# Forgetting attention rewritten as 64 steps of one row tile of two heads, with a fixed order on three engines

## The chip, the cores and the metric

The kernel runs on one core of a Trainium2 chip, as a single launch. The metric is the device time of that launch in microseconds (us). The core has the engines TensorE (PE, with its weight loads shown apart as PEld), VectorE (DVE), ScalarE (ACT) and GpSimd (POOL), and SyncE (SP), which here issues transfers. ACT and POOL issue transfers too. Each engine works through its own instructions in order and waits on semaphores for the others.

## The reference, cut to what matters

The whole computation is a two-layer decoder trunk on 1024 tokens of 1024 features, in float32: an RWKV-7 layer and a mixture of experts, then a "forgetting attention" layer and a second mixture of experts. The change lies in the attention layer, which has 16 heads of 64 features:

```
for i in range(S // Q_BLOCK):                       # 8 blocks of 128 rows
    lo, hi = i * Q_BLOCK, (i + 1) * Q_BLOCK
    logits = (einsum('bhqd,bhkd->bhqk', q[:, :, lo:hi], k[:, :, :hi]) * scale
              + (fcum[:, :, lo:hi, None] - fcum[:, :, None, :hi]))
    causal = (lo + arange(Q_BLOCK))[:, None] >= arange(hi)[None, :]
    logits = where(causal, logits, -inf)
    p = softmax(logits, axis=-1)
    outs.append(einsum('bhqk,bhkd->bhqd', p, v[:, :, :hi]))
...
return (o * sigmoid(qg[..., D:])) @ w_o             # w_o is scaled by (1 + gt_m) afterwards
```

Row block i sees (i + 1) * 128 keys, so the work of a block grows eightfold from i = 0 to i = 7.

## The kernel before

The eight head pairs (`m` = 0 to 7, two heads `e` each) are worked one after another; a pair has two halves of four row blocks. For one row block of one head (`Attention.half`, lines 2119 to 2159):

- PE multiplies the queries with the keys (L2138, two passes that add a high and a low part) and adds the causal mask (L2141), into a PSUM tile `psc`, of which there are two (two banks each). This is called S below.
- DVE adds the forget sums `nf` to it, writes the logits into `lg` and takes the row minimum in the same instruction (L2144; the scores are negated, so the minimum is the maximum). This is called L. A tiny instruction subtracts and adds the row's own forget sum to that minimum (L2150).
- ACT takes the exponential with that minimum as bias, and the row sum (L2151).
- DVE takes the reciprocal of the sum (L2152) and scales the row (L2153).
- PE transposes the row in 128 x 128 tiles (L2158) into the PSUM tiles `ptr` (three of one bank), called T, and ACT copies them out to `pT` (L2159).

When two row blocks of both heads are done, PE multiplies `pT` with `v` (L2170, called V), which adds up in `po` (one bank); after two such groups DVE multiplies by the output gate into `oT` (L2174). `lg` has four buffers, `nf` three, `v` one, `pT` two for each head.

In the pairs m = 1 to 4, after each half, `Attention.weight` prepares one of eight 128-row blocks of the output weights: a transfer into `wor`, which takes one of the four `lg` buffers, POOL multiplies it by the gate row (L2186), ACT copies it to `woh` (L68) and POOL subtracts to `wol` (L69).

Nothing fixes the order by hand: the framework's list scheduler lays the instructions of the five engines out by its own estimate of time, and each engine then works through its list. Queries and keys are loaded from the POOL queue, `v`, `nf`, gates and weights from the SP queue. Ahead of the attention the gates are computed (`Qkv.gates`): their sigmoid tiles `gs` lie in a pool that is closed before the attention's pool, with `lg` in it, is opened in the same memory. Behind it `out1` multiplies `oT` with the weights.

## Time and profile before

| | us |
|---|---|
| median of 3 runs (3153.26 to 3163.05) | 3161.29 |
| the profiled execution | 3158.01 |
| its span | 3156.3 |
| PE, DVE, ACT, POOL busy over the span | 2885.3, 2409.2, 1701.7, 853.9 |
| the attention, from the first logits (2074.67) to the end (2357.50) | 282.83 |
| PE, PEld, DVE, ACT, POOL busy in it | 256.01, 179.47, 213.21, 191.47, 83.20 |

The attention is 9% of the span. The mean granted TensorE clock over the span is 0.949 of 2.4 GHz. A record of a matmul holds its way through the pipeline too, so records of neighbours overlap, and how fast PE gets through a row of them is read from the starts of the weight loads. An idle time in square brackets stands before the instruction, with what ended it.

### The profile page before, as it was taken

To read this page: it belongs to the slowest core of one execution; us is meant where nothing else is said; L and a number is where in the kernel's file an instruction comes from. 1 tells how busy PE (TensorE), PEld (TensorE's weight loads), DVE (VectorE), ACT (ScalarE), POOL (GpSimd) and SP (SyncE) were. 2 spreads that over 40 slices of the span, in tenths; PEclk is the share of its full clock that TensorE was granted. 3 is DMA by queue.
4 is the path that set the end of the run, shared out by engine and by line. 5 is a ranking of instruction groups with operands and counts; after the bars stand their busy time and mean duration, and the time that the engine had idled before them with its cause. 6 is when DMAs were issued, how large, how long until landed. Compare 5 with 4: busy or idle time off the path is not lost. (4 is left out here: it accounts for less than half of the span.)

```text
span 3156.3 us, 51219 instructions
## 1 busy us (share of the span) xinstructions
PE 2885.3 (91%) x19763; PEld 2209.3 (70%) x19763; DVE 2409.2 (76%) x3676; ACT 1701.7 (54%) x2563; POOL 853.9 (27%) x446
## 2 busy tenths in 40 slices
PE   7989997769997999999989999998999799999996
PEld 5658776657775677767758989865667577766773
DVE  7477558478777999999965544167767899999996
ACT  4432554333334777767754233256663477776774
POOL 4010316000002344444400033023303532224430
PEclk9989998689998999999999999999999899999998
DMA  6487673485534999999975745546644399999995
GB/s 207 143 269 248 207 233 109 117 174 133 134 104 180 374 383 390 376 349 361 384 288 174 221 138 204 164 120 159 173 103 181 129 388 388 383 365 348 367 380 222
DMA packets 362035, 771.12 MB, mean 244 GB/s; under 512 B 134723, under 2 KB 236315, under 8 KB 311742
## 3 DMA queue, kind: packets, MB, share of 16 engines
q1 hardware_dynamic: 277596, 630.23, 57.6%
q0 software_dynamic: 29104, 70.55, 7.6%
q10 hardware_dynamic: 55090, 67.04, 6.6%
q8 instruction: 157, 2.57, 0.3%
q14 instruction: 88, 0.72, 0.1%
HBM read 664.06 MB, written 120.18 MB: 248 GB/s over the span
## 5 line engine op out<-in xcount | busy, mean ns | idle before, releaser
L1392 DVE TENSOR_TENSOR mlo<-mraw,mhi 128x1024 fp32r<-128x1024 f32 x752 | 872.8, 1218 | 13.2 <-ACT mhi L1387 12.7
L1387 ACT ACTIVATE mhi<-mraw 128x1024 fp32r<-128x1024 f32 x752 | 748.4, 1052 | 190.3 <-PE pd L1484 97.3
L1364 POOL DMA_INDIRECT Yd<-yo,sidx x64 | 396.1, 6189 | 422.9 <-DVE yo L1512 415.4
L1936 PE MATMUL ptk<-wh,hhi 128*128 128x256 f32 x768 | 216.7, 289 | 10.8 <-ACT ksq L1948 6.3
L1936 PE MATMUL ptk<-wl,hhi 128*128 128x256 f32 x768 | 215.9, 285 | 0.0
L1484 PE MATMUL pg<-mhi,xTl 128*96 128x512 f32 x512 | 205.2, 401 | 4.9 <-DVE xTl L69 4.9
L1484 PE MATMUL pd<-mhi,hTh 128*96 128x512 f32 x512 | 207.8, 406 | 0.0
L1936 PE MATMUL ptk<-wh,hlo 128*128 128x256 f32 x768 | 207.3, 286 | 0.2 <-DVE hlo L69 0.2
L1484 PE MATMUL pg<-mhi,xTh 128*96 128x512 f32 x512 | 205.1, 401 | 0.5 <-ACT xTh L68 0.5
L1484 PE MATMUL pu<-mhi,xTh 128*96 128x512 f32 x512 | 204.6, 400 | 0.0
L1484 PE MATMUL pd<-mhi,hTl 128*96 128x512 f32 x512 | 204.4, 399 | 0.0
L1484 PE MATMUL pd<-mlo,hTh 128*96 128x512 f32 x512 | 203.4, 397 | 0.0
L1484 PE MATMUL pg<-mlo,xTh 128*96 128x512 f32 x512 | 203.2, 397 | 0.0
L1484 PE MATMUL pu<-mhi,xTl 128*96 128x512 f32 x512 | 202.2, 395 | 0.0
L1484 PE MATMUL pu<-mlo,xTh 128*96 128x512 f32 x512 | 201.3, 393 | 0.2 <-POOL mlo L69 0.2
L1936 PEld LDWEIGHTS ptk<-wh,hhi 128*128 128x128 f32 x768 | 146.9, 193 | 16.2 <-ACT ksq L1948 8.0
L1358 POOL DMA_INDIRECT xb<-Hd,gidx x64 | 75.7, 1183 | 283.8 <-PE pxt L1471 279.9
L2144 DVE CUSTOM_DVE_ANT_0 lg<-psc,nf 128x256 f32<-128x256 f32 (+7 forms) x128 | 95.3, 752 | 74.0 <-DMA G1d<-gs 44.9
L1936 PEld LDWEIGHTS ptk<-wl,hhi 128*128 128x128 f32 x768 | 148.2, 193 | 0.3 <-issue 0.2
L1936 PEld LDWEIGHTS ptk<-wh,hlo 128*128 128x128 f32 x768 | 142.8, 193 | 2.3 <-issue 1.7
L1512 DVE SCALAR_TENSOR_TENSOR yo<-pd,gtab,mgt 96x512 f32<-96x512 f32 x128 | 93.2, 742 | 28.4 <-PE pd L1484 27.8
L1484 PEld LDWEIGHTS pg<-mhi,xTl 128*96 128x96 f32 x512 | 83.8, 164 | 43.6 <-DVE xTl L69 7.0
(555 smaller groups left out, 6920.4 us busy)
## 6 DMA issues: line engine op xcount, KB each, us to landing
mraw<-in_moe_wgate_dram SPq DMA_DIRECT2D x128, 1024.0 KB
mraw<-in_moe_wup_dram SPq DMA_DIRECT2D x128, 1024.0 KB
mraw<-in_moe_wdown_dram SPq DMA_DIRECT2D x128, 1024.0 KB
adaw<-in_ada_w_dram SPq DMA_DIRECT2D x48, 512.0 KB
mraw<-in_ada_w_dram SPq DMA_DIRECT2D x32, 512.0 KB
Q<-Qd POOLq DMA_DIRECT2D x64, 256.0 KB, 5.7
adk<-in_ada_w_dram SPq DMA_DIRECT2D x16, 512.0 KB
adaw<-in_kv_ada_w_dram SPq DMA_DIRECT2D x16, 512.0 KB
```

What stands on the lines that cost most here:

```text
L1358: return g.nc.gpsimd.indirect_dma_start(out=X[0:SL], out_offset=None, in_=g.Hd[l][:, :], in_offset=bass.IndirectOffsetOnAxis(ap=idx[0:SL], ...
L1364: return g.nc.gpsimd.indirect_dma_start(out=g.Yd[l][:, :], out_offset=bass.IndirectOffsetOnAxis(ap=idx[0:SL], axis=0), in_=Yo[0:SL], in_of ...
L1387: self.ex.g.nc.scalar.activation(hi, raw, AF.Copy)
L1392: self.ex.g.nc.vector.tensor_tensor(lo, raw, hi.bitcast(F32), op=ALU.subtract)
L1484: self.g.nc.tensor.matmul(p, a[:, k, :], b[:, kk, s], start=(k == 0 and j == 0), stop=(k == n - 1 and j == len(tt) - 1))
L1512: self.g.nc.vector.scalar_tensor_tensor(yo[0:SL, s], p, gcol[0:SL], self.gt[0:SL, s], op0=ALU.mult, op1=ALU.mult)
L1936: nc.tensor.matmul(p[:, 0:KU], x[:, t * P:(t + 1) * P], w[:, k, :], start=(k == 0 and j == 0), stop=(k == KT - 1 and j == 2))
L2144: nc.vector.tensor_tensor_reduce(lg[:, 0:W].rearrange("p (s w) -> p s w", s=ns), sc[:, 0:ns, 0:w], nf[e][:, 0:W].rearrange("p (s w) -> p s ...
```

## The change

The attention becomes one loop over 64 steps (`Attention.run`). A step is one row block of both heads of a pair. Within `Order`, the instructions of PE, ACT and DVE keep the order in which the program writes them. A step works on its own block `u` and on the block of the step before, `before`:

- PE: S of both heads of `u`, T of `before`'s first head, half of a waiting V, T of `before`'s second head.
- ACT: the copies of `before`'s first head, both exponentials of `u`, the copies of `before`'s second head.
- DVE: a gate product that is due, L of both heads of `u`, one piece of the weights, then reciprocal and scaling of each head of `u`.

The subtract-and-add of the forget sum (old L2150) is gone; the exponential takes the minimum as it comes. The weights are gated and split on DVE (instead of POOL), with the copy still on ACT, one block in five steps, in parts of `oT` that are not written yet. `nf` has four buffers, `v` two; the sigmoid tiles of the gates take the slots of the attention's gate tiles. A triangle of ones for the forget sums moves into a scratch area. Everything ahead of the gates and behind the attention has its order unchanged, but for a few of the last rows of the program.

```diff
         self.load_q(m, 0)
-        v = lp.tile([P, NT, P], F32, name="v1")
-        nc.sync.dma_start(v, g.V1d[:, m * P:(m + 1) * P].rearrange("(t p) c -> p t c", p=P))
         nf = []
         for e in range(2):
-            n_ = lp.tile([P, T], F32, name="nf", bufs=3)
+            n_ = lp.tile([P, T], F32, name="nf", bufs=4)
             nc.sync.dma_start(n_, brow(g.Fd[2 * m + e:2 * m + e + 1, :], T))
             nf.append(n_)
-        self.k[m] = K, v, nf
+        self.k[m] = K, nf
+
+    def load_v(self, m):
+        self.v[m] = (self.lp, self.sp)[m % 2].tile([P, NT, P], F32, name="v1")
+        self.g.nc.sync.dma_start(self.v[m], self.g.V1d[:, m * P:(m + 1) * P].rearrange("(t p) c -> p t c", p=P))
...
+    def run(self, sp, ps, oT):
+        g = self.g
+        order = Order(g.tc, mybir.EngineType.PE, mybir.EngineType.Activation, mybir.EngineType.DVE)
+        self.sp, self.ps, self.oT = sp, ps, oT
+        before, side = None, self.weights()
+        self.load_v(0)
+        for m in range(KT):
+            for half in range(2):
...
+                for ii in range(4):
+                    if ii == 0:
+                        group = Ctx()
+                        group.gt, group.m, group.half = gt, m, half
+                    u = Ctx()
+                    u.m, u.half, u.ii, u.i, u.group = m, half, ii, half * 4 + ii, group
+                    with order:
+                        self.step(u, before, side)
+                    before = u
+        while before or self.todo or self.gated:
+            with order:
+                self.step(None, before, side)
+            before = None
+        assert next(side, 1)
+
+    def step(self, u, before, side):
+        if self.gated:
+            self.gated()
+            self.gated = None
+        if u:
+            for e in range(2):
+                self.scores(u, e)
+            for e in range(2):
+                self.logits(u, e)
+            next(side, None)
+        if before:
+            self.transposed(before, 0)
+        if u:
+            self.exponents(u, 0)
+        if self.todo:
+            self.todo.pop(0)()
+        if u:
+            self.exponents(u, 1)
+            for e in range(2):
+                self.scaled(u, e)
+        if before:
+            self.transposed(before, 1)
+            if before.ii % 2:
+                for part in range(2):
+                    self.todo.append(lambda part=part: self.values(before, part))
+
...
-                    lg = sp.tile([P, T], F32, name="lg", bufs=4)
-                    mx = sp.tile([P, 4], F32, name="mx", bufs=4)
-                    nc.vector.tensor_tensor_reduce(
-                        lg[:, 0:W].rearrange("p (s w) -> p s w", s=ns), sc[:, 0:ns, 0:w],
-                        nf[e][:, 0:W].rearrange("p (s w) -> p s w", s=ns), 1.0, 3.0e38, op0=ALU.add, op1=ALU.min,
-                        accum_out=mx[:, 0:1])
-
-                    ft = g.fc[:, i, h:h + 1]
-                    nc.vector.tensor_scalar(mx[:, 1:2], mx[:, 0:1], ft, ft, op0=ALU.subtract, op1=ALU.add)
-                    nc.scalar.activation(lg[:, 0:W], lg[:, 0:W], AF.Exp, bias=mx[:, 1:2], scale=-1.0, accum_out=mx[:, 2:3])
-                    nc.vector.reciprocal(mx[:, 3:4], mx[:, 2:3])
-                    nc.vector.tensor_scalar(lg[:, 0:W], lg[:, 0:W], mx[:, 3:4], None, op0=ALU.mult)
-                    for j0 in range(0, i + 1, 4):
-                        n = min(4, i + 1 - j0)
-                        p = ps.tr.tile([P, 4, P], F32, name="ptr")
-                        for j in range(n):
-                            nc.tensor.transpose(p[:, j, :], lg[:, (j0 + j) * P:(j0 + j + 1) * P], g.ident)
-                        nc.scalar.activation(pT[:, j0:j0 + n, iq * P:(iq + 1) * P], p[:, 0:n], AF.Copy)
...
+    def exponents(self, u, e):
+        lg, mx = u.lg[e]
+        self.g.nc.scalar.activation(lg[:, 0:u.W], lg[:, 0:u.W], AF.Exp, bias=mx[:, 0:1], scale=-1.0, accum_out=mx[:, 2:3])
+
+    def scaled(self, u, e):
+        lg, mx = u.lg[e]
+        self.g.nc.vector.reciprocal(mx[:, 3:4], mx[:, 2:3])
+        self.g.nc.vector.tensor_scalar(lg[:, 0:u.W], lg[:, 0:u.W], mx[:, 3:4], None, op0=ALU.mult)
+
+    def transposed(self, u, e):
+        g, nc, lg = self.g, self.g.nc, u.lg[e][0]
+        if u.ii % 2 == 0 and e == 0:
+            self.pT = [self.sp.tile([P, NT, 256], F32, name=f"pT{x}", bufs=2) for x in range(2)]
+        u.pT = self.pT
+        s = slice(u.ii % 2 * P, u.ii % 2 * P + P)
+        for j0 in range(0, u.i + 1, 4):
+            n = min(4, u.i + 1 - j0)
+            p = self.ps.tr.tile([P, 4, P], F32, name="ptr")
+            for j in range(n):
+                nc.tensor.transpose(p[:, j, :], lg[:, (j0 + j) * P:(j0 + j + 1) * P], g.ident)
+            nc.scalar.activation(u.pT[e][:, j0:j0 + n, s], p[:, 0:n], AF.Copy)
+
...
+        for j in range(part * nj // 2, (part + 1) * nj // 2):
             t0 = max(0, j - nj + 2) * P
...
-            self.gate = sp.tile([P, D], F32, name="gate1")
-            nc.sync.dma_start(self.gate, brow(g.modr[M_GT1:M_GT1 + 1], D))
-            nc.gpsimd.tensor_scalar(self.gate, self.gate, 1.0, None, op0=ALU.add)
-        raw = sp.tile([P, D], F32, name="wor", tag="lg", bufs=4)
-        nc.sync.dma_start(raw, g.I["fx_wo"][0, k * P:(k + 1) * P, :])
-        nc.gpsimd.tensor_tensor(raw, raw, self.gate, op=ALU.mult)
-        w = [self.bp.tile([P, D], F32R, name=n, tag="hl", bufs=16) for n in ("woh", "wol")]
-        split(g, *w, raw, nc.gpsimd)
-        self.wo.append(w)
+        gate = self.oT[:, KT - 1]
+        nc.sync.dma_start(gate, brow(g.modr[M_GT1:M_GT1 + 1], D))
+        for k in range(KT):
+            hi, lo = (self.bp.tile([P, D], F32R, name=n, tag="hl", bufs=16) for n in ("woh", "wol"))
+            raw = self.oT[:, KT - 2 - (k % 2 and k < KT - 1)]
+            nc.sync.dma_start(raw, g.I["fx_wo"][0, k * P:(k + 1) * P, :])
+            self.wo.append([hi, lo])
+            yield
+            yield
+            if k == 0:
+                nc.vector.tensor_scalar(gate, gate, 1.0, None, op0=ALU.add)
+            nc.vector.tensor_tensor(raw, raw, gate, op=ALU.mult)
+            yield
+            nc.scalar.activation(hi, raw, AF.Copy)
+            yield
+            nc.vector.tensor_tensor(lo, raw, hi.bitcast(F32), op=ALU.subtract)
+            yield
...
-            with tc.tile_pool(name="gp", bufs=1) as sp:
-                for u in range(4):
-                    q.gates(sp, 12 + u, u)
-                    q.load()
+            for u in range(4):
+                q.gates(lp, 12 + u, u)
+                q.load()
...
-            for m in range(KT):
-                for half in range(2):
-                    if half == 0:
-                        at.load_q(m, 1)
-                    elif m + 1 < KT:
-                        at.load(m + 1)
-                    at.half(sp, ps, oT, m, half)
-                    if 1 <= m < 5:
-                        at.weight(sp, (m - 1) * 2 + half)
-            while at.late:
-                at.values(sp, ps, *at.late.pop(0))
+            at.run(sp, ps, oT)
```

ACT in the fourth pair (m = 3), from the exponentials of the row block with 640 keys. Before (`lg` logits, `pT` transposed rows, `woh` high part of the output weights):

```order
L2151 ACTIVATE lg,mx<-lg,mx 128x640 x2
L2159 ACTIVATE pT_20733<-ptr 128x4x128
L2159 ACTIVATE pT_20835<-ptr 128x4x128
L2159 ACTIVATE pT_20835<-ptr 128x128
L68 ACTIVATE woh<-wor 128x1024
L2151 ACTIVATE lg,mx<-lg,mx 128x768 x2
L2159 ACTIVATE pT_20836<-ptr 128x4x128
L2159 ACTIVATE pT_20836<-ptr 128x128
```

The same stretch now, up to the next weight copy:

```order
L2204 ACTIVATE lg,mx<-lg,mx 128x640 x2
L2222 ACTIVATE pT_20326<-ptr 128x4x128
L2222 ACTIVATE pT_20423<-ptr 128x4x128
L2222 ACTIVATE pT_20423<-ptr 128x128
L2204 ACTIVATE lg,mx<-lg,mx 128x768 x2
L2222 ACTIVATE pT_20424<-ptr 128x4x128
L2222 ACTIVATE pT_20424<-ptr 128x128
L2222 ACTIVATE pT_20423<-ptr 128x4x128
L2222 ACTIVATE pT_20423<-ptr 128x2x128
L2204 ACTIVATE lg,mx<-lg,mx 128x896 x2
```

The copy `woh` stood between two row blocks' exponentials and read what POOL had written; it now stands one block further on, ahead of the copies of the step, and reads what DVE wrote in the step before.

DVE at the last two row blocks of a pair. Before, in m = 5 (`mx` the minimum, the sum and its reciprocal, `g` the gate):

```order
L2144 ISA lg,mx<-psc,nf 128x896
L2144 ISA mx 128x1
L2150 TENSOR_SCALAR mx<-mx,fc 128x1
L2144 ISA lg,mx<-psc,nf 128x1024
L2144 ISA mx 128x1
L2150 TENSOR_SCALAR mx<-mx,fc 128x1
L2152 RECIPROCAL mx<-mx 128x1
L2150 TENSOR_SCALAR mx<-mx,fc 128x1
L2153 TENSOR_SCALAR lg<-lg,mx 128x896
```

Now, in m = 3, a step with a weight product in it (`oTt` on its own is the weight block):

```order
L2196 ISA lg,mx<-psc,nf 128x896
L2196 ISA mx 128x1
L2254 TENSOR_TENSOR oTt<-oTt 128x1024
L2208 RECIPROCAL mx<-mx 128x1
L2209 TENSOR_SCALAR lg<-lg,mx 128x896
L2208 RECIPROCAL mx<-mx 128x1
L2209 TENSOR_SCALAR lg<-lg,mx 128x896
L2237 TENSOR_TENSOR oTt<-po,g_20183 128x512
L2196 ISA lg,mx<-psc,nf 128x1024
```

Before, the logits of the next block stood between the logits and the scaling of this one. Now the scaling of both heads of a block comes before any logits of the next, and the weight product stands between the two.

PE at the row block with 896 keys. Before, in m = 6 (`psc` scores, `ptr` transposes, `po` values):

```order
L2138 MATMUL psc<-K_21619,Q_21860 128x384 x4
L2141 LDWEIGHTS identbf
L2141 MATMUL psc<-cmask,identbf 128x128
L2158 MATMUL ptr<-ident,lg 128x128 x12
L2170 MATMUL po<-pT_21930,v_21627 64x256
L2158 MATMUL ptr<-ident,lg 128x128
L2138 MATMUL psc<-K_21617,Q_21857 128x448 x4
L2141 LDWEIGHTS identbf
L2141 MATMUL psc<-cmask,identbf 128x128
L2170 MATMUL po<-pT_21931,v_21627 64x256
L2170 MATMUL po<-pT_21930,v_21627 64x256
```

Now, one step in m = 6:

```order
L2185 MATMUL psc<-K_21494,Q_21703 128x448 x4
L2188 LDWEIGHTS identbf
L2188 MATMUL psc<-cmask,identbf 128x128
L2221 MATMUL ptr<-ident,lg 128x128 x6
L2234 MATMUL po<-pT_21845,v_21506 64x256
L2234 MATMUL po<-pT_21846,v_21506 64x256
L2234 MATMUL po<-pT_21845,v_21506 64x128
L2234 MATMUL po<-pT_21846,v_21506 64x128
L2221 MATMUL ptr<-ident,lg 128x128 x6
L2185 MATMUL psc<-K_21492,Q_21700 128x512 x4
```

Scores, transposes of one head, values, transposes of the other head now follow one another in every step, where single value products and transposes stood between the scores before.

## Rows read from the trace of the kernel before

**Rows 1.** Windows, pairs m = 1 to 6; us, then PE, PEld, DVE, ACT, POOL busy, clock, DMA, GB/s

```profile
2101.04:2135.93 34.89, 33.68 (x242) 24.31 (x242) 27.74 (x87) 26.07 (x62) 10.71 (x12) 1.00 0.72 184
2135.93:2170.79 34.86, 30.56 (x210) 20.93 (x209) 28.61 (x79) 23.76 (x57) 15.79 (x14) 1.00 0.58 162
2170.79:2215.02 44.23, 34.95 (x218) 24.79 (x217) 26.83 (x82) 24.50 (x59) 15.59 (x14) 0.88 0.64 156
2215.02:2253.46 38.44, 33.09 (x218) 22.94 (x217) 29.21 (x82) 24.54 (x59) 16.08 (x14) 0.96 0.61 158
2253.46:2286.06 32.60, 30.50 (x208) 20.79 (x206) 25.02 (x81) 22.47 (x56) 11.17 (x12) 1.00 0.65 159
2286.06:2318.93 32.87, 30.47 (x212) 21.60 (x212) 24.55 (x82) 22.66 (x56) 4.88 (x8) 0.95 0.71 160
...
sum 282.83, PE 256.01 PEld 179.47 DVE 213.21 ACT 191.47 POOL 83.20; mean PE 32.00 PEld 22.43 DVE 26.65 ACT 23.93 POOL 10.40
```

**Rows 2.** Waits in the attention: who waited for whom, us in total, times, longest us

```profile
ACT woh L68 <- POOL wor L2186: 27.2, 8, 6.2
```

**Rows 3.** Timeline in pair m = 3: start, us, engine, what; idle before

```profile
2199.30 1.06 ACT L68 ACTIVATE woh<-wor 128x1024 fp32r<-128x1024 f32 x1 [4.25 <-POOL wor L2186]
2201.50 1.71 DVE L2153 TENSOR_SCALAR lg<-lg,mx 128x768 f32<-128x768 f32 x1
...
2203.32 1.14 PEld L2158 LDWEIGHTS ptr<-ident,lg 128*128 128x128 f32 x6 [4.84 <-ACT pT L2159]
```

**Rows 4.** Timeline at the start of the attention, ACT

```profile
2074.59 1.28 ACT L2151 ACT_TABLE_LOAD   x1 [2.33 <-DMA G1d<-gs]
```

**Rows 5.** Timeline in pair m = 2, PE's weight loads and one scaling

```profile
2155.01 1.49 PEld L2170 LDWEIGHTS po<-pT,v 128*64 128x64 f32 x14 [0.17 <-issue]
...
2162.10 0.61 DVE L2153 TENSOR_SCALAR lg<-lg,mx 128x768 f32<-128x768 f32 x1
...
2164.00 0.64 PEld L2158 LDWEIGHTS ptr<-ident,lg 128*128 128x128 f32 x6 [0.39 <-issue]
...
2164.61 0.76 PEld L2138 LDWEIGHTS psc<-K,Q 128*128 128x128 f32 x4
...
2165.65 0.10 PEld L2141 LDWEIGHTS <-identbf 128*128 128x128 bf16 x1 [0.28 <-issue]
...
2166.17 2.35 PEld L2170 LDWEIGHTS po<-pT,v 128*64 128x64 f32 x22
...
2174.62 0.30 PEld L2138 LDWEIGHTS psc<-K,Q 128*128 128x128 f32 x2 [1.54 <-DVE mx L2144]
...
2174.97 0.10 PEld L2141 LDWEIGHTS <-identbf 128*128 128x128 bf16 x1
```

**Rows 6.** Timeline in pair m = 7, PE's weight loads behind values

```profile
2327.21 0.14 PEld L2158 LDWEIGHTS ptr<-ident,lg 128*128 128x128 f32 x1 [0.38 <-issue]
```

**Rows 7.** Groups of instructions in the attention: busy us, mean ns, idle before

```profile
L2151 ACT ACTIVATE lg<-lg,mx 128x256 f32<-128x256 f32 (+7 forms) x128 | 98.6, 773 | 21.2 <-DVE mx L2150 15.5 <-DVE mx L2152 5.0
L2144 DVE CUSTOM_DVE_ANT_0 lg<-psc,nf 128x256 f32<-128x256 f32 (+7 forms) x128 | 95.3, 752 | 74.0 <-DMA G1d<-gs 44.9 <-PE ptr L2158 21.5 <-PE psc L2141 3.8
L2170 PE MATMUL po<-pT,v 128*64 128x256 f32 (+1 forms) x640 | 89.9, 373 | 9.8 <-DMA v<-V1d 5.3 <-ACT pT L2159 4.1
L2153 DVE TENSOR_SCALAR lg<-lg,mx 128x256 f32<-128x256 f32 (+7 forms) x128 | 77.2, 606 | 1.7
L2150 DVE TENSOR_SCALAR mx<-mx,fc 128x1 f32<-128x1 f32 x128 | 33.1, 266 | 0.8
L2152 DVE RECIPROCAL mx<-mx 128x1 f32<-128x1 f32 x128 | 20.2, 159 | 20.5 <-ACT lg L2151 19.7
L2174 DVE TENSOR_TENSOR oTt<-po,g 128x512 f32<-128x512 f32 x16 | 11.0, 688 | 17.5 <-PE po L2170 17.5
L68 ACT ACTIVATE woh<-wor 128x1024 fp32r<-128x1024 f32 x8 | 8.5, 1058 | 27.2 <-POOL wor L2186 27.2
```

**Rows 8.** Page, groups: a product of two 128 x 1024 tiles on DVE

```profile
L1392 DVE TENSOR_TENSOR mlo<-mraw,mhi 128x1024 fp32r<-128x1024 f32 x752 | 872.8, 1218 | 13.2 <-ACT mhi L1387 12.7
```

100 lines of the change are left out of this document (50 added, 50 removed).

## The prediction

> **What bounds the kernel now.** I read the windows of the attention first, one for each head pair. The reader is to see two kinds of pair [rows 1]. m = 5 and 6, in which no weights are prepared, take 32.60 and 32.87 us, and PE is busy in 30.5 of each. The four with weights take 34.89, 34.86, 44.23 and 38.44, 152.4 together, though PE and DVE have no more attention to do: against four pairs of 32.7 that is 21.6 us more. Eight pairs of 32.7 and these 21.6 make 283.2, which is the stretch's 282.83. So there are two quantities to work out, a pair without weights and the weights.
>
> The table of waits says what the weights cost: ACT stood 27.2 us in front of its eight copies `woh`, waiting for POOL [rows 2]. The timeline shows what that does to others [rows 3]. ACT idles 4.25 us before one `woh`, with the exponentials of the next row block queued behind it; PE's transposes then come 4.84 us late, and the six of them take 1.14 us where six take 0.64 elsewhere [rows 5], because the granted clock had fallen to 1.2 GHz in the idle time. The window of that pair has a mean clock of 0.88 [rows 1].
>
> The start is in the timeline too: the table load for the first exponential waits 2.33 us for the transfer that empties `gs` [rows 4], since `lg` lies in the memory of `gs`.
>
> **The change, part by part.**
>
> *PE in a pair.* The three kinds of work are the same as before, so I price them by the spacing of the weight loads where PE waits for nobody [rows 5]. T: 0.64 / 6 = 0.107 us a tile; a head has 36 tiles, a pair 72: 7.7 us. V: 2.35 / 22 = 0.107 a record; the 320 products show as 640 records [rows 7], 80 a pair: 8.6 us, or 0.9 less if the narrow products on the diagonal take half. S: for 512 columns from 2174.62 to 2174.97 + 0.10 = 0.45 us, for 2048 from 2164.61 to 2165.65 + 0.10 = 1.14. A line through both, over the 9,472 columns of a head's eight blocks, gives 8 x 0.45 + 5,376 x 0.45 / 1000 = 6.0, and 12.0 a pair. Together 28.3. The new order goes once in each step from T to V and once back. The first costs 0.17 [rows 5]; the second costs 0.38 in the one row I have [rows 6], and I let it go down to the 0.17 of the first: 8 x 0.34 to 8 x 0.55, 2.7 to 4.4. A pair then needs 31.0 to 32.7 of PE alone. I take 31.5, a little below the middle, since the upper end rests on that one row: 252 us for eight. A pair without weights gains only about 1.2 us by this.
>
> *DVE and ACT in a step.* The tiny instruction after L goes: 128 x 266 ns = 33.1 us of records [rows 7]; on DVE they overlap their neighbours, so it is worth less there, but in the chain of a row it stood in front of the exponential, and ACT waited 15.5 us for it. The new chain on DVE in a step is L, both exponentials, a reciprocal and the second scaling. Per pair, from the groups: 95.3 / 16 + 98.6 / 8 + 20.2 / 16 + the scaling. The scaling's 77.2 holds instructions slowed beside POOL, such as the 1.71 us for 768 columns [rows 3] that take 0.61 otherwise [rows 5]. POOL's sixteen products go, at most 1.1 us each, 17.6; I take 10, near the middle between none and that, so 67 / 16. With the gate product, 11.0 / 8, that is 6.0 + 12.3 + 1.3 + 4.2 + 1.4 = 25.2. Three handovers a step show no price of their own; between nothing and 0.17 each they add up to 4.1. So the chain needs 25 to 29 a pair, and PE's 31.5 lies above it: PE is the bound, if it gets to work a step ahead.
>
> The Trainium skill says on the page "SBUF — State Buffer", section "SBUF: two separate sides", that GpSimd and VectorE share a port pair as an exclusive lock and that the loser blocks for the whole instruction. By that rule all sixteen products held a scaling up and 17.6 come back; DVE would then have room for all of the weights, and the time would be 3133 instead of the 3139 below. The 1.71 is one such case; the 606 ns mean of the group is too low for every product to have cost a full one, so I keep 10.
>
> *The weights.* They leave POOL. ACT's 27.2 us of waiting goes, and with it the 21.6 us worked out above. What is late next is their work on DVE: sixteen products of 1.22 [rows 8] and one scalar addition, which at 0.61 x 1024 / 768 is 0.8: 20.3 us; ACT keeps its 8 x 1.06 = 8.5. If all of it lay on the path it would cost 28.8, if PE hides it nothing. It is spread over 40 steps, five pairs. PE's 31.5 leaves the middle of the chain, 27, about 4.5 a pair: 22.5 of room for 28.8. I take 6 on the path. On DVE the scalings are queued behind a product, and PE's transposes of the next step wait for those; a late transfer of a weight block would hold the whole step. Its issue lies eight steps ahead of its product from the third block on, at 3 to 4 us a step; of the first two blocks the product comes two and seven steps after, so one stall of a few us at the start is possible and is inside the bound.
>
> *Start and end.* With `gs` out of the way the first exponential comes 2.3 us earlier [rows 4]; the gates' last sigmoids on ACT and the last gate matmuls are then what is late. `nf` and `v` with one more buffer take away 5.3 us of PE's wait for `v` [rows 7]; that is inside the 32.7 and so inside the gain of a pair. Filling and emptying the pipeline of steps adds what PE waits in the first and last one: between 0 and 10, about three chains of 3.3; I take 5. Moving the triangle costs nothing: POOL makes it in both, far ahead of its use. Behind the attention the order is the same but for the last rows of the program; I cost that at 0, within 1 us.
>
> *Sum.* 252 + 6 + 5 = 263 against 282.8, that is 19.8 less, and 2.3 at the start: 22.1. The profiled execution took 3158.0 (span 3156.3), which becomes 3135.9. The median of the runs lies 3.3 above the profiled one: 3139.
>
> **The rivals.**
>
> *Everything hides (faster still).* Switches cost 0.17 each, narrow V products take half, the weights cost nothing, ends 2: 30.1 x 8 + 2 = 243, 42 less with the start, so 3119. For it: a steady order gives PE no long idle time, so the clock stays at 2.4 GHz. Against it: S, T and V would never wait for one another, and in the pairs without weights today PE still idles 2 us by its records [rows 1].
>
> *The weights only change engines (no change).* In a fixed order a product on DVE or a copy on ACT delays the scaling and so the next transposes each time, and all 28.8 lie on the path: 252 + 29 + 5 = 286, less 2.3, so 3162. For it: in a step with a product the chain (27 / 8 + 1.2 = 4.6) is longer than PE's mean step (31.5 / 8 = 3.9). Against it: the product stands where DVE waits for the exponential anyway.
>
> *PE never gets ahead (slower).* On ACT the exponentials of a step are queued behind the copies of the step before, those wait for transposes, and these stand on PE behind both scores of the step. The old list put the next block's logits into DVE's gaps; the new one can't. If PE starts a step's scores only when DVE is ready for them, a step's chain gets longer by one score, one head's transposes and a copy. By the rows that is 6.0 + 3.9 + 8 x 0.5 = 14 a pair; in half of the steps 7: 27 + 7 = 34 a pair, 272 + 29 + 5 = 306, 21 more with the start, so 3182. It decides from the point where ACT stands more than 0.6 us a step before its first copy. For it: ACT and DVE take their queues strictly in order, and [rows 3] shows a chain behind one late instruction. The skill's page "TensorE: Matmul & The Clock Gate", section on the array's architecture, says the same of both queues and that only PE can pull weight loads ahead; the trace agrees with the 4.84 us. Against it: two `psc` let PE run the next scores as soon as this step's logits are done, well ahead of the scalings.
>
> **How the numbers follow.** A change under 0.3%, 9.5 us, can't be told from none here. Forecast (12 to 32 us less) 0.53, everything hides 0.20, only change engines 0.15, never ahead 0.12. So faster 0.73, same 0.15, slower 0.12. The range goes from 3116, below the best case, to 3160, just short of the no-change case: it leaves out the slower case and part of the one before it.
>
> **What would show it.** Right: no wait of `woh` for POOL; PE's weight loads in a pair without weights spaced to 31 to 32 us; pairs with weights within 2 us of the others; the first logits 2 to 3 us after the last gate matmul; a granted clock of 1.0 in all pairs. Wrong: ACT idle before copies in most steps (never ahead); the first five pairs 4 us or more longer than the last three (only change engines); DVE waiting for a weight block's transfer; or a pair at 29 us or less, which would mean that today's spacing of PE's groups is not its floor.

## The result, and the profile after

The changed kernel takes 3115.32 us, the median of 4 runs (3110.18 to 3115.52), against 3159.8 for the kernel before beside it (4 runs, 3153.26 to 3163.05): ratio 0.9861, 95% interval 0.9843 to 0.9879. The forecast was 3139 with a range from 3116; the gain is twice the one forecast. The profiled execution took 3115.35 us (span 3113.6) against 3158.01: 42.7 less. The attention, from the first logits to the end of the last gate product, gives 36.7 of it, 246.15 against 282.83.

Lines move with the change: scores are L2185, the mask L2188, logits L2196, exponentials L2204, reciprocal and scaling L2208 and L2209, transposes L2221 and their copies L2222, products with v L2234, the gate product L2237, the weights L2253 to L2258. The first view is the windows of the eight pairs of the changed kernel, with the columns of [rows 1].

```profile
2071.99:2102.21 30.22, 24.96 (x165) 18.00 (x164) 25.96 (x69) 24.14 (x56) 6.14 (x10) 0.94 0.67 183
2102.21:2132.68 30.47, 29.01 (x219) 20.58 (x218) 25.91 (x70) 24.00 (x59) 6.00 (x10) 1.00 0.83 194
2132.68:2162.68 30.00, 29.18 (x218) 20.60 (x217) 25.91 (x71) 24.38 (x59) 6.14 (x10) 1.00 0.88 212
2162.68:2192.72 30.04, 29.28 (x219) 20.64 (x217) 25.97 (x70) 23.64 (x58) 5.97 (x10) 1.00 0.79 193
2192.72:2222.95 30.23, 28.66 (x217) 20.34 (x216) 26.88 (x71) 24.35 (x58) 6.01 (x11) 1.00 0.92 191
2222.95:2252.67 29.72, 29.01 (x220) 20.59 (x218) 23.10 (x67) 22.84 (x57) 5.75 (x10) 1.00 0.77 177
2252.67:2281.99 29.32, 28.81 (x218) 20.45 (x217) 23.13 (x68) 22.68 (x57) 4.59 (x8) 1.00 0.82 171
2281.99:2318.14 36.15, 34.31 (x265) 24.77 (x263) 23.76 (x68) 24.77 (x60) 0.21 (x2) 1.00 0.08 15
sum 246.15, PE 233.24 PEld 165.98 DVE 200.62 ACT 190.80 POOL 40.80; mean PE 29.15 PEld 20.75 DVE 25.08 ACT 23.85 POOL 5.10
```

Every pair but the last now takes nearly the same, 29.3 to 30.5, where [rows 1] ran from 32.60 to 44.23; the last one, 36.15, also holds the emptying of the pipeline. The pairs with weights are 0.7 longer than those without. The granted clock is at 1.0 in all but the first. Next, five lines of the table of waits in the changed kernel, from just ahead of the attention (who waited for whom, us in total, times, longest).

```profile
DVE lg L2196 <- PE psc L2188: 49.3, 14, 42.1
ACT pT L2222 <- PE ptr L2221: 43.3, 67, 1.2
DVE mx L2208 <- ACT lg L2204: 25.6, 54, 2.1
PE ptr L2221 <- DVE mx L2208: 7.4, 8, 2.0
ACT lg L2204 <- DVE mx L2196: 6.1, 15, 0.8
```

The wait of ACT for `woh` is gone from the table (27.2 us in [rows 2]), and in the attention no engine waits for a transfer any more. PE's own waits are brief. Of the first line, 42.1 us are the one wait for the first scores of all; the other 13 waits, 7.2 us, come back below. The scalings, L2209, are the row that answers to the 77.2 of [rows 7]:

```profile
L2209 DVE TENSOR_SCALAR lg<-lg,mx 128x256 f32<-128x256 f32 (+7 forms) x128 | 67.0, 524 | 4.5
```

The start, where [rows 4] had 2.33 us for the transfer out of `gs`; the table load now follows the last gate's sigmoid at once:

```profile
2071.34 1.08 ACT L2057 ACTIVATE gs<-pft 128x512 f32<-128x512 f32 x2 [9.79 <-PE pft L1996]
...
2072.82 1.28 ACT L2204 ACT_TABLE_LOAD   x1 [0.40 <-ACT gs L2057]
```

### The profile page after: what moved, and what is told of

It is laid out like the page before. It is cut to its first block, busy times and chain, and to the rows that moved or that the text cites. A ratio compares the mean times of both kernels' runs of the same rounds, so it can differ in the third digit from the quotient of the medians.

```text
span 3113.6 us, 51077 instructions
## 1 busy us (share of the span) xinstructions
PE 2861.3 (92%) x19763; PEld 2194.2 (70%) x19763; DVE 2394.0 (77%) x3565; ACT 1700.5 (55%) x2563; POOL 807.0 (26%) x429
## 3 DMA queue, kind: packets, MB, share of 16 engines
q1 hardware_dynamic: 277596, 630.23, 58.7%
## 5 line engine op out<-in xcount | busy, mean ns | idle before, releaser
L1364 POOL DMA_INDIRECT Yd<-yo,sidx x64 | 389.1, 6079 | 424.2 <-DVE yo L1512 412.5
L1932 PEld LDWEIGHTS ptk<-wh,hhi 128*128 128x128 f32 x768 | 145.1, 191 | 13.8 <-ACT ksq L1944 6.4
L2196 DVE CUSTOM_DVE_ANT_0 lg<-psc,nf 128x256 f32<-128x256 f32 (+7 forms) x128 | 91.6, 752 | 49.3 <-PE psc L2188 49.3
L1512 DVE SCALAR_TENSOR_TENSOR yo<-pd,gtab,mgt 96x512 f32<-96x512 f32 x128 | 93.2, 743 | 28.9 <-PE pd L1484 28.4
```

What stands on the lines that cost most here:

```text
L1364: return g.nc.gpsimd.indirect_dma_start(out=g.Yd[l][:, :], out_offset=bass.IndirectOffsetOnAxis(ap=idx[0:SL], axis=0), in_=Yo[0:SL], in_of ...
L1512: self.g.nc.vector.scalar_tensor_tensor(yo[0:SL, s], p, gcol[0:SL], self.gt[0:SL, s], op0=ALU.mult, op1=ALU.mult)
L1932: nc.tensor.matmul(p[:, 0:KU], x[:, t * P:(t + 1) * P], w[:, k, :], start=(k == 0 and j == 0), stop=(k == KT - 1 and j == 2))
L2196: self.g.nc.vector.tensor_tensor_reduce(lg[:, 0:u.W].rearrange("p (s w) -> p s w", s=u.ns), u.sc[e][:, 0:u.ns, 0:u.w], self.k[u.m][1][e][: ...
```

## The experiments

Most of these kernels ran once, and the time ahead of the attention differs between executions (first logits anywhere from 2061 to 2080 us), so what is compared is the attention alone, in one profiled execution of each. The changed kernel gave 246.15 and, in a second execution (e15_after_again), 245.95; e16_early_gate_timed is e12_early_gate once more. "With" is the mean of the pairs m = 1 to 4, "without" the pairs m = 5 and 6, cut at the first logits of a pair in all kernels; times in us.

| kernel | time of the profiled execution | attention | with | without |
|---|---|---|---|---|
| before | 3158.01 | 282.83 | 38.11 | 32.60, 32.87 |
| changed | 3115.35 | 246.15 | 30.19 | 29.72, 29.32 |
| e6_noscale | 3109.77 | 233.70 | 28.57 | 28.52, 28.52 |
| e5_v_twice | 3161.42 | 295.30 | 36.14 | 35.87, 36.09 |
| e4_tiny | 3176.21 | 304.80 | 37.94 | 36.48, 34.56 |
| e4b_tiny2 | 3144.79 | 272.36 | 33.88 | 32.05, 31.87 |
| e7_v_whole | 3119.86 | 245.97 | 30.59 | 29.31, 29.16 |
| e2_noweights | 3099.76 | 241.72 | 29.31 | 29.30, 29.18 |
| e1_pool | 3138.07 | 261.89 | 32.32 | 29.59, 29.30 |
| e9_old_vec | 3162.30 | 296.65 | 39.88 | 33.93, 34.22 |
| e3_noorder | 3137.50 | 266.67 | 32.09 | 30.78, 30.73 |
| e10_bufs | 3171.28 | 302.44 | 39.24 | 36.48, 37.64 |
| e14_old_bufs | 3156.90 | 279.57 | 38.60 | 31.67, 30.25 |
| e8_old_no_tiny | 3159.63 | 289.31 | 39.96 | 33.78, 30.95 |
| e11_early | 3123.95 | 254.02 | 31.27 | 30.78, 30.67 |
| e12_early_gate | 3118.74 | 244.04 | 30.06 | 28.65, 29.04 |
| e13_early_gate_whole | 3123.10 | 246.43 | 30.57 | 29.47, 29.46 |
| e15_after_again | 3121.99 | 245.95 | 30.19 | 29.73, 29.17 |
| e16_early_gate_timed | 3120.24 | 244.58 | 30.06 | 28.65, 29.03 |
| e17_early_split | 3114.25 | 240.56 | 29.51 | 28.64, 29.02 |

**What a pair hangs on.** Theory: PE's own work. Rival: the chain over DVE and ACT. Four kernels lengthen or shorten one of the two.

First e6_noscale, then e5_v_twice:

```diff
 def scaled(self, u, e):
-    self.g.nc.vector.tensor_scalar(lg[:, 0:u.W], lg[:, 0:u.W], mx[:, 3:4], None, op0=ALU.mult)
...
 def values(self, u, part):
...
-            for e in range(2):
+            for e in (0, 1, 0, 1):
...
```

> The changed kernel without the scaling by the reciprocal (its reciprocals stay), so rows are not normalised. Theory (PE is the bound): pairs without weights stay at 28.9 to 29.4 although DVE loses 4.2 us in each; pairs with weights fall to the same, attention 240 to 245. Rival (the chain is the bound): pairs 2 to 4 us shorter, attention 214 to 230.

> The changed kernel with each product with v made twice (the sums in po are doubled): 80 more PE records a pair. Theory (PE is the bound, and V costs 0.093 a record, half for narrow ones): a pair without weights goes from 29.3 to 36.0 to 37.0, attention 300 to 310. The price of the prediction, 0.107 a record: 37.9, attention 313 to 318. Rival (the chain over DVE and ACT is the bound, PE has 4 us of room a pair): pairs at 31.5 to 34, attention 262 to 285.

Windows of m = 5 and 6 in e6_noscale, then the same two in e5_v_twice:

```profile
2213.42:2241.94 28.52, 28.52 (x219) 20.29 (x218) 15.17 (x51) 22.30 (x57) 5.75 (x10) 1.00 0.84 185
2241.94:2270.46 28.52, 28.51 (x219) 20.29 (x218) 15.18 (x51) 22.29 (x57) 4.59 (x8) 1.00 0.86 181
```

```profile
2247.57:2283.44 35.87, 35.87 (x297) 25.62 (x295) 23.35 (x67) 22.41 (x57) 5.75 (x10) 1.00 0.64 145
2283.44:2319.53 36.09, 36.09 (x298) 25.82 (x297) 23.44 (x66) 22.62 (x57) 4.59 (x8) 1.00 0.66 145
```

In both PE is busy from end to end, pair after pair the same: that is PE alone, 28.52 with V once and 36.1 with V twice. The difference, 7.5 us for 80 records, prices V at 0.094 a record, as the theory of e5_v_twice had it, though its attention of 295.30 lies a little below the theory's range. e6_noscale falls between its two ranges: a pair gets 0.8 to 1.2 shorter, neither nothing nor 2 to 4. So the changed kernel's 29.3 (29.7 in m = 5) stands 0.8 or more above PE's floor: PE is nearly its bound but not quite. What holds it up shows when the chain is lengthened. This is e4_tiny; in e4b_tiny2 the first two added lines stand at the end of `logits`.

```diff
 def exponents(self, u, e):
     lg, mx = u.lg[e]
-    self.g.nc.scalar.activation(lg[:, 0:u.W], lg[:, 0:u.W], AF.Exp, bias=mx[:, 0:1], scale=-1.0, accum_out=mx[:, 2:3])
+    ft = self.g.fc[:, u.i, 2 * u.m + e:2 * u.m + e + 1]
+    self.g.nc.vector.tensor_scalar(mx[:, 1:2], mx[:, 0:1], ft, ft, op0=ALU.subtract, op1=ALU.add)
+    self.g.nc.scalar.activation(lg[:, 0:u.W], lg[:, 0:u.W], AF.Exp, bias=mx[:, 1:2], scale=-1.0, accum_out=mx[:, 2:3])
```

> The changed kernel with the subtract-and-add of one column between the logits and the exponential put back. Theory (PE is the bound of a pair): it hides, pairs longer by 0.5 us at most, time 3114 to 3120. Rival (the chain over DVE and ACT is the bound): 64 steps longer by 0.2 to 0.5 us, 13 to 32 us, time 3128 to 3147.

> As e4_tiny, but each subtract-and-add stands right behind its own logits, as in the kernel before, and not behind both logits and the weights' product. Theory (PE is the bound, and e4_tiny's 58 us came from the first exponential no longer running beside the second logits): two instructions of 0.27 us a step fit beside PE, attention 246 to 252 against 246.15. Rival (the chain has no room: any instruction in it costs its length): 64 steps of 0.25 to 0.5 us, attention 262 to 278.

Both theories priced e4_tiny too low: 58.7 us more. There the tiny instruction stands on DVE behind both logits and the weights' product, so the first exponential no longer runs beside them; ACT waits 79.9 us for it. With it right behind its own logits (e4b_tiny2) a pair still takes 2.3 to 2.6 more, for eight steps with two of them: the rival's answer, for PE's own work did not grow. The steps don't share it evenly. From one step's first logits to the next's, in m = 5, the steps of 128 and 256 columns take 3.04 each in both kernels; those of 384 and 512 get 0.2 longer, the four widest 0.3 to 0.6. ACT's waits in e4b_tiny2, where the changed kernel has 6.1 for the logits:

```profile
ACT lg L2206 <- DVE mx L2201: 31.9, 57, 1.4
```

So in the wide steps the bound of the changed kernel is a ring, and the timeline shows it: one step of m = 5, row tile 5 (768 columns), first DVE and then ACT.

```profile
2239.39 0.95 DVE L2196 CUSTOM_DVE_ANT_0 lg<-psc,nf 128x768 f32<-128x768 f32 x1
2240.27 0.08 DVE L2196 DVE_READ_ACCUMULATOR2_ANT mx<- 128x1 f32 x1
2240.27 0.95 DVE L2196 CUSTOM_DVE_ANT_0 lg<-psc,nf 128x768 f32<-128x768 f32 x1
...
2241.71 0.62 DVE L2209 TENSOR_SCALAR lg<-lg,mx 128x768 f32<-128x768 f32 x1
2242.43 0.17 DVE L2208 RECIPROCAL mx<-mx 128x1 f32<-128x1 f32 x1
2242.63 0.62 DVE L2209 TENSOR_SCALAR lg<-lg,mx 128x768 f32<-128x768 f32 x1
2243.16 1.08 DVE L2196 CUSTOM_DVE_ANT_0 lg<-psc,nf 128x896 f32<-128x896 f32 x1
```

```profile
2240.45 0.94 ACT L2204 ACTIVATE lg<-lg,mx 128x768 f32<-128x768 f32 x1 [0.21 <-DVE mx L2196]
2241.29 0.19 ACT L2204 ACTIVATION_READ_ACCUMULATOR lg<-lg,mx 128x1 f32 x1
2241.38 0.92 ACT L2204 ACTIVATE lg<-lg,mx 128x768 f32<-128x768 f32 x1
2242.21 0.19 ACT L2204 ACTIVATION_READ_ACCUMULATOR lg<-lg,mx 128x1 f32 x1
```

First logits, first exponential, second exponential, second reciprocal, second scaling, and then the next step's first logits, each starting when the one before it lets go: 3.77 us round. In the narrow steps it is PE that leads. In the same pair the first logits of 256 and of 384 columns stand idle until PE has made their scores, so the steps of 128 and 256 columns are as long as PE makes them:

```profile
2225.99 0.42 DVE L2196 CUSTOM_DVE_ANT_0 lg<-psc,nf 128x256 f32<-128x256 f32 x1 [0.63 <-PE psc L2188]
...
2229.03 0.56 DVE L2196 CUSTOM_DVE_ANT_0 lg<-psc,nf 128x384 f32<-128x384 f32 x1 [0.72 <-PE psc L2188]
```

That is why a pair is longer than PE alone needs, and why no single engine is full in it.

**Switches between T and V on PE** (e7_v_whole).

```diff
-                for part in range(2):
-                    self.todo.append(lambda part=part: self.values(before, part))
+                self.todo.append(lambda: [self.values(before, part) for part in range(2)])
```

> The changed kernel with the products of a pair of row tiles in one piece every second step, and not in halves in every step: four switches from T to V and back fewer in a pair. Theory (PE is the bound and a switch costs what the gaps between its weight loads show, 0.17 and 0.17 to 0.39): pairs without weights at 27.0 to 28.2, attention 230 to 240. Rival (with the products in lumps PE falls behind in one step and waits in the next): pairs at 29.3 to 31, attention 246 to 258.

The theory's gain does not come: the attention is the same. The steps have become uneven, as the rival has it (in m = 5 the first two take 2.33 and 4.26, where they took 3.04 each), but the sum stays at the rival's lower end. PE's busy time in m = 5 and 6 falls from 29.01 and 28.81 to 28.26 and 28.37, 0.6 a pair for eight switches, 0.07 each. That is likely too low: PE does not set the pace here, and a record ahead of an idle stretch holds some of that. The starts of the matmuls in e6_noscale, where PE never waits, give a switch more exactly. Weight loads, then matmuls, in m = 5:

```profile
2230.14 0.63 PEld L2233 LDWEIGHTS po<-pT,v 128*64 128x64 f32 x8 [0.17 <-issue]
2231.15 0.53 PEld L2220 LDWEIGHTS ptr<-ident,lg 128*128 128x128 f32 x5 [0.39 <-issue]
```

```profile
2229.49 0.72 PE L2220 MATMUL ptr<-ident,lg 128*128 128x128 f32 x5
2230.14 1.08 PE L2233 MATMUL po<-pT,v 128*64 128x256 f32 x8
2231.15 0.77 PE L2220 MATMUL ptr<-ident,lg 128*128 128x128 f32 x5
```

Within a row of its kind a transpose starts 0.109 after the one before it, a wide V product 0.108, a narrow one 0.055. Five transposes would so take 0.55 and eight wide products 0.86; from start to start they take 0.65 and 1.01. The two switches cost 0.10 and 0.15, where the loader idled 0.17 and 0.39: its idle time is not the array's. Over the pair, by the same starts, S takes 10.84, 72 transposes at 0.109 make 7.85, V makes 7.78, and of the 28.52 there are 2.05 left for sixteen switches, 0.13 each.

The transposes' records run to 2230.21, beyond the start of V's loads, and V's to 2231.22, beyond that of the next loads. The Trainium skill ("TensorE: Matmul & The Clock Gate", section "Step-by-step: what each phase is for") says that weight loads are pulled ahead of matmuls under way while the matmuls stay in order; the two views agree with it.

**The weights.**

In e2_noweights the whole work of `weights` gives way to two loads a block, with its five yields kept:

```diff
+            for w in (hi, lo):
+                nc.gpsimd.dma_start(w, g.I["fx_wo"][0, k * P:(k + 1) * P, :].bitcast(F32R))
```

In e1_pool its three DVE instructions change engine:

```diff
-                nc.vector.tensor_scalar(gate, gate, 1.0, None, op0=ALU.add)
-            nc.vector.tensor_tensor(raw, raw, gate, op=ALU.mult)
+                nc.gpsimd.tensor_scalar(gate, gate, 1.0, None, op0=ALU.add)
+            nc.gpsimd.tensor_tensor(raw, raw, gate, op=ALU.mult)
...
-            nc.vector.tensor_tensor(lo, raw, hi.bitcast(F32), op=ALU.subtract)
+            nc.gpsimd.tensor_tensor(lo, raw, hi.bitcast(F32), op=ALU.subtract)
```

> The changed kernel with no weights made in the attention: the two halves are loaded by DMA as they are, so gating and splitting of the output weights are left out. Theory (PE hides most of the weights; pairs with them are 0.7 us longer than those without): attention 241 to 245, time 3109 to 3114. Rival 1 (all of the 28.8 us of weights lies on the path): time 3084 to 3092. Rival 2 (all hidden): no difference beyond 1 us, time 3114 to 3117.

> The changed kernel with the weights' seventeen products and eight subtractions back on POOL, at the same places in the new order. Theory (the place in the queues is what mattered: a product stands a whole step ahead of ACT's copy of it): copies woh wait under 2 us in all, the pairs m = 1 to 4 stay at 29.5 to 31, attention 244 to 250, time 3112 to 3121; only the scalings grow, from 67 us towards 77. Rival (the engine is what mattered, by its speed and by the port it shares with DVE): ACT waits 10 us or more for POOL, pairs with weights 33 to 38, time 3128 to 3137.

Without weights the pairs m = 1 to 6 take 29.2 to 29.3 and the attention 4.4 us less, as the theory has it. On POOL (seventeen instructions in all, the eight subtractions among them), at the same places in the queues, it takes 15.7 more, nearly half of it in m = 0 (37.57 against 30.22). That is the rival's time, but not its way: the copies `woh` wait only once, 1.2 us, and the pairs m = 1 to 4 stay at 31.3 to 33.0. The loss is on DVE, whose scalings take 21.6 more than in the changed kernel:

```profile
L2209 DVE TENSOR_SCALAR lg<-lg,mx 128x256 f32<-128x256 f32 (+7 forms) x128 | 88.6, 692 | 4.5
```

POOL and then DVE, early in m = 0 of e1_pool:

```profile
2084.39 2.35 POOL L2254 TENSOR_TENSOR oTt<-oTt 128x1024 f32<-128x1024 f32 x1
2086.70 1.25 POOL L2114 DMA_DIRECT2D Q<-Qd  x2
2087.97 2.35 POOL L2254 TENSOR_TENSOR oTt<-oTt 128x1024 f32<-128x1024 f32 x1
2090.26 1.21 POOL L2114 DMA_DIRECT2D Q<-Qd  x2
2091.49 2.35 POOL L2258 TENSOR_TENSOR wol<-oTt,woh 128x1024 fp32r<-128x1024 f32 x1
```

```profile
2084.94 2.02 DVE L2209 TENSOR_SCALAR lg<-lg,mx 128x384 f32<-128x384 f32 x1
...
2087.07 7.00 DVE L2209 TENSOR_SCALAR lg<-lg,mx 128x384 f32<-128x384 f32 x1
```

A scaling of 384 columns takes 7.00 us and ends only when POOL does, through two tensor instructions and the transfer issues between them; one of 512 columns takes 0.49 soon after, at 2095.81. The Trainium skill ("SBUF — State Buffer", section "SBUF: two separate sides") has the loser of the shared port pair blocked for one whole instruction; here it was blocked for a whole run of them, so the measured loss is larger than the rule's 2.35.

And the other way round, in the kernel before (e9_old_vec):

```diff
-            nc.gpsimd.tensor_scalar(self.gate, self.gate, 1.0, None, op0=ALU.add)
+            nc.vector.tensor_scalar(self.gate, self.gate, 1.0, None, op0=ALU.add)
...
-        nc.gpsimd.tensor_tensor(raw, raw, self.gate, op=ALU.mult)
+        nc.vector.tensor_tensor(raw, raw, self.gate, op=ALU.mult)
...
-        split(g, *w, raw, nc.gpsimd)
+        split(g, *w, raw, nc.vector)
```

> The kernel before, with one edit: the weights' products and subtractions on DVE instead of POOL, where the old order has them. Theory (most of the weights' 21.6 us came from POOL's slow turn and from the port it shares with DVE): pairs with weights at 33.5 to 35.5, attention 266 to 274. Rival (they came from the places in the queues: ACT's copy and DVE's product wait in front of the row chain whichever engine makes the product): attention 276 to 286.

Worse than the rival's range: 13.8 us more than before. In the old order a raw block lies in a buffer of the logits, and DVE stands in front of its transfer with logits queued behind:

```profile
DVE wor L2186 <- DMA wor<-in_fx_wo_dram: 19.6, 8, 5.4
```

So DVE alone is no cure. In the changed kernel the raw blocks lie in rows of `oT` that are not yet written, are asked for two steps ahead and more, and no such wait is left. No run moved the raw blocks alone, so what their place is worth by itself stays open.

**Order, buffers, and the tiny instruction by themselves.**

First e3_noorder (the same in the second place where `step` is called), then e10_bufs, then e8_old_no_tiny, an edit of the kernel before, in which the exponential also takes `mx[:, 0:1]` as its bias; e14_old_bufs takes the hunks of the change on `tri1`, `gs`, `nf` and `v` alone and puts the gate row into `oT[:, KT - 1]`.

```diff
-                    with order:
-                        self.step(u, before, side)
+                    self.step(u, before, side)
```

```diff
-            n_ = lp.tile([P, T], F32, name="nf", bufs=4)
+            n_ = lp.tile([P, T], F32, name="nf", bufs=3)
-        self.v[m] = (self.lp, self.sp)[m % 2].tile([P, NT, P], F32, name="v1")
+        self.v[m] = self.lp.tile([P, NT, P], F32, name="v1")
```

```diff
-                    ft = g.fc[:, i, h:h + 1]
-                    nc.vector.tensor_scalar(mx[:, 1:2], mx[:, 0:1], ft, ft, op0=ALU.subtract, op1=ALU.add)
...
```

> The changed kernel without the fixed order: the same instructions and buffers, with the scheduler free to move them on PE, ACT and DVE. Theory (the steady order is what brings a pair from 32.7 to 29.5): pairs m = 5 and 6 at 31.5 to 33.5, attention 260 to 272, time 3128 to 3141. Rival (the shorter chain and the buffers did it, the order nothing): pairs at 29 to 30.5, time 3112 to 3119.

> The changed kernel with the buffers of before: three for nf and one for v. Theory (a load that has to wait for the last reader comes late in the next pair, and in a fixed order nothing else runs meanwhile): 2 to 5 us more in each of seven pairs, attention 258 to 280. Rival (the loads are short enough to hide): attention 245 to 249.

> The kernel before with the changed kernel's memory alone: four buffers for nf, two for v, gs in the memory of g1, the triangle and the gate row moved to make room; order, weights on POOL and the subtract-and-add as before. Theory (the old list has other work while a load is late, so the buffers bring little by themselves): the start 2 to 3 us earlier, attention 272 to 283. Rival (the buffers are the gain, the order only its use): attention 255 to 268.

> The kernel before, with one edit: the subtract-and-add of one column is gone and the exponential takes its bias from the logits' minimum. Theory (each row's chain over DVE and ACT paces the old order too, so the tiny instruction stood on the path): pairs m = 5 and 6 go from 32.7 to 30 to 31.5, attention 262 to 272. Rival (the prediction's: on DVE it overlaps its neighbours, about 1 us a pair at most): attention 274 to 283.

Without the fixed order the attention is 20.5 longer: 14.4 in m = 0 and 1 (36.46 and 38.68), where the weights as the scheduler places them stall ACT (8.7 us for products) and DVE (7.0 us for their transfers), 4.2 in the last pair, and 1.9 in the rest. So the theory's total comes, but not by its way: a pair without weights takes 30.75, so that of the 3.2 us which such a pair gains, the fixed order gives 1.2 and the rest of the change 2.0. With the old buffers and the fixed order the attention is 56.3 longer, more than the theory's range and worse than the kernel before:

```profile
DVE lg L2196 <- DMA nf<-Fd: 36.0, 7, 6.8
```

Each of the seven changes of pair waits some 5 us for `nf`, and on DVE nothing behind it may go; PE waits 10.1 us more for `v`. In m = 3 PE idles 4.29 us behind the late logits and 3.90 for `v`, and as it goes on the granted clock is at 1.2 GHz both times: the pair takes 44.28 us at a mean of 0.85, where the changed kernel has 30.04 at 1.0. The kernel before, with the same buffers, waited 2.9 us for `nf` and 5.3 for `v`; that its list had other work to put there is the likely reason, not a shown one. Its order with the new buffers (e14_old_bufs) gains 3.3, as the theory has it. Without the tiny instruction (e8_old_no_tiny) it loses 6.5, outside both ranges: the edit gives another list, in which m = 1 takes 40.98 instead of 34.89 and m = 6 takes 30.95 instead of 32.87, so the old order can't tell what one instruction costs.

**Opening the ring.** `after` is the next step's tile, whose first head's scores and logits leave the start of its own step. In e12_early_gate and the kernels behind it the three lines on `gated` stand here too; in e11_early they stay at the step's start.

```diff
             self.exponents(u, 1)
-            for e in range(2):
-                self.scaled(u, e)
+            self.scaled(u, 0)
+        if self.gated:
+            self.gated()
+            self.gated = None
         if before:
             self.transposed(before, 1)
...
+            if after:
+                self.scores(after, 0)
+                self.logits(after, 0)
+            self.scaled(u, 1)
```

> The changed kernel with one move: the next step's first scores and logits are issued one place earlier, so that on DVE these logits stand in front of the reciprocal and scaling of this step's second head; PE's and ACT's orders stay. Theory (in the changed kernel a step hangs on a ring: first logits, both exponentials, second scaling, next first logits; PE alone needs 28.5 a pair): the ring opens and PE sets the pace, pairs without weights 28.4 to 28.8 and with weights at most 0.5 more, attention 234 to 239. Rival (the second scaling now waits for PE's scores and comes late for the transposes): pairs at 29.5 to 32, attention 247 to 262.

> As e11_early, with the gate product moved too: it stands behind the first scaling of the step that ends its sums, and not behind the next step's early logits and the second scaling, where PE's next sums waited 26 us for it (there is one po). Theory (the ring over DVE and ACT is what holds a pair at 29.3; opened, PE's 28.5 is the bound): pairs without weights 28.4 to 29.0, attention 234 to 241. Rival (the early logits make the second scaling wait for PE's scores, and the ring comes back through PE): pairs 29.5 to 31, attention 246 to 254.

> As e12_early_gate, with the products with v in one piece every second step. Theory (PE is then the bound, and four switches each way cost 0.17 to 0.39): pairs without weights 26.8 to 27.8, attention 224 to 233. Rival (lumps on PE, as in e7_v_whole, make DVE's early logits wait in one step and PE in the next): pairs at 28.5 to 31, attention 236 to 254.

e11_early lost 7.9: PE stood 16.5 us in front of the one `po` until its gate product was done.

```profile
PE po L2243 <- DVE oTt L2246: 16.5, 15, 1.4
```

With that product moved (e12_early_gate) pairs without weights reach 28.65 and 29.04, close to PE's floor of 28.52, as the theory has it; those with weights stay at 30.06, and the last pair takes 37.41 where it took 36.15. So only 2.1 us of the attention are gained, and its 244.04 lies between the two ranges. V in one piece brings nothing here either (e13_early_gate_whole, 246.43, its edit that of e7_v_whole): PE is less busy, 27.95 a pair, but waits 7.6 us for the second scalings and 8.4 for the copies.

> The changed kernel itself, timed beside the two below. Both theories: attention 245 to 248, ratio to the kernel before 0.984 to 0.988.

> e12_early_gate, timed. Theory (the opened ring keeps what one execution showed): attention 242 to 246, ratio 0.001 below the changed kernel's, 1 to 4 us; too little to tell surely. Rival: no difference or slower, ratio equal or above.

> e12_early_gate with the weights' products, copies and subtractions in halves of 512 columns, spread over more steps. Theory (the weights cost 4 us because a product of 1.2 us stands between the logits and the scalings): pairs with weights fall from 29.7 to 30.4 towards 28.7 to 29.3, attention 238 to 242, ratio 0.982 to 0.986. Rival (more instructions cost what the shorter ones save): attention 243 to 247.

In e17_early_split each instruction on a weight block becomes two of this form, `h` the two halves of 512 columns, one a step:

```diff
-            nc.vector.tensor_tensor(raw, raw, gate, op=ALU.mult)
+            nc.vector.tensor_tensor(raw[:, h[0]], raw[:, h[0]], gate[:, h[0]], op=ALU.mult)
+            yield
+            nc.vector.tensor_tensor(raw[:, h[1]], raw[:, h[1]], gate[:, h[1]], op=ALU.mult)
```

The three timed beside the kernel before (5 runs each, 9 of before): the changed kernel 0.9858 (0.9832 to 0.9883), early logits 0.9833 (0.9809 to 0.9856), and with weights in halves 0.9845 (0.9822 to 0.9868). The intervals overlap, so whole times don't tell them apart. The attention does: 245.95, 244.58 and 240.56; in halves the weights cost 0.55 a pair less (29.51, where the theory had 28.7 to 29.3), and this is the shortest attention of a kernel that leaves nothing out. Its median is 3112.27, against 3117.24 for the changed kernel; the early logits alone had 3108.6, though their attention is 4 us longer, so the medians order by what lies outside of it.

## Why the prediction was wrong

The direction was right, and so were most parts; the gain was priced at half. For the attention 263 was forecast and 246.15 measured, 16.9 less. For the whole kernel 3139 was forecast and 3115.32 measured, nearly 24 less: 16.9 in the attention, 0.4 at the start, 3.3 behind the attention, and 3.3 by which the runs' median was to lie above the profiled execution and did not. The last two are not shown to be the change's.

*PE in a pair, the step that failed.* 31.5 was forecast and the pair takes 29.3: 8 x 2.2 = 17.6 us, a little more than the whole miss in the attention. PE alone, the 31.5 of the forecast, needs 28.52 (e6_noscale). T was right, 7.7 forecast and 7.85 measured. S was put at 12.0 and takes 10.84, in good part because the forecast counted the mask's load, 0.10, in full at the end of each of the sixteen blocks, where the next matmul starts 0.04 to 0.07 after the mask's. V was put at 8.6, with "0.9 less if the narrow products on the diagonal take half"; they do (0.055 against 0.108), and V takes 7.8 by its starts, 7.5 by e5_v_twice. The switches were put at 2.7 to 4.4, 3.2 in the 31.5, from gaps between weight loads [rows 5, 6], and take 2.05. All three errors went one way: edges were priced from the loader's records. The view for it was there, the starts of PE's matmuls beside those of its loads.

*The chain on DVE and ACT, 25 to 29, and "PE is the bound".* The chain of the forecast is the ring, and its price was about right: a pair of 29.3 to 29.7 lies just above the range, and 0.63 and 0.72 of it, in m = 5, are waits for PE. What failed is the comparison. The forecast set the sum of a pair for PE against that for the chain and took the longer one. But PE leads in the narrow steps and the ring in the wide ones, so the pair takes longer than either alone: 0.8 or more above PE's 28.52, and above the ring's 28.4, an estimate from m = 5, its 29.72 less those two waits.

*The tiny instruction.* It was costed as worth less than its 33.1 us. Put back into the new order it costs 26.2, so that was right; by the steps, it costs nothing where PE leads and its whole length in the widest (0.6 us for two of 0.27).

*The weights.* 6 on the path were forecast, 4.4 measured, and the old 21.6 are gone. Their cause was told too simply: with DVE alone the old order gets 13.8 worse (e9), on POOL the new order 15.7 worse (e1). It takes the engine and the new order together; that the raw blocks' place counts too is read from e9's 19.6 us of waiting and not shown by itself.

*Scalings.* 10 us were to come back from POOL: 77.2 became 67.0, 10.2, and not the 17.6 of the rival rule. It depends on the order: in the new one the same work on POOL costs the scalings 21.6 (e1).

*Buffers.* "Inside the 32.7 and so inside the gain of a pair" was half the truth: in the old order they bring 3.3, but the fixed order stands on them, 56.3.

*Start and end.* The start was put at 2.3; DVE's wait for its first logits went from 44.9 to 42.1, 2.8 less. Filling and emptying: 5 forecast; without weights the attention is 241.72, that is 8 x 29.3 + 7.3. With the pair's 17.6 and the weights' 1.6 less, and these 2.3 more, 263 becomes 246.1. Behind the attention the two profiled executions differ by 3.3 us (798.8 and 795.5), which is not shown to be the change: kernels with the old order had 794.4 to 796.0 there.

*The rivals.* "Everything hides" (30.1 a pair, 3119) came nearest, and mostly by its mechanism: cheap switches, narrow products at half, the clock at 1.0; but the weights cost 4.4 and not nothing, and even its pair was too long. "Only change engines" asked for 28.8 on the path. "PE never gets ahead" needs ACT idle for 0.6 us a step before its copies: its waits before all copies are 43.3 / 64 = 0.68, past that point, and yet no pair comes near that rival's 34. ACT is busy for only 22.8 of 29.5 and has that time to spare; the point was put too low.

## What to carry to other kernels

Price TensorE's work and its switches from the starts of its matmuls, not from the records of its loader. Before saying what bounds a steady loop, walk its ring once round through all engines, across the step's edge, and do it for each size of step: an instruction in the ring costs its length where the ring leads and nothing where another engine does, and a loop whose steps differ can take longer than any one engine needs for the whole. A fixed order wants its loads early and buffers to hold them, since nothing goes round a late one; judge order, buffers and the placing of side work together, for one by one they may each lose.

## What the runs showed of the hardware

A DVE scaling of 384 columns, 0.42 us in most others of its size, took 7.00 beside a run of POOL instructions, longer than any one of them. A change between transposes and the 64-row products cost TensorE 0.13 us on average, about half of what its weight loads showed as idle. After TensorE had idled 4.29 and 3.90 us in m = 3 of e10_bufs, the granted clock was at 1.2 GHz as it went on. The attention of one program repeats closely (246.15 and 245.95 for the changed kernel; 244.04 and 244.58 for the early logits, these on two chips), while the time ahead of it moves by much more (first logits at 2071.99 and 2077.80 in the two executions of the changed kernel).
